# Router logits with the router's weights held in TensorE in two column tiles and the tokens streaming

## The chip, the cores and the metric

The kernel runs on one core of one Trainium2 chip. The metric is the time of one execution on the device, in microseconds (us), as the median of several runs.

## What is computed

One layer of a decoder trunk for 256 tokens of 2048 channels in fp32: two token mixers, a cross-attention into 256 memory tokens, a mixture of 32 experts, and a final norm. The part that matters here is the router ahead of the experts:

```python
p_grp = jax.nn.softmax((hn @ w_rg + b_rg), axis=-1)          # 4 groups
g_top = jnp.argmax(p_grp, axis=-1)
e_logits = (hn @ w_re + b_re).reshape(-1, N_GROUPS, EXPERTS_PER_GROUP)   # 32 experts
e_in = jnp.take_along_axis(e_logits, g_top[:, None, None], axis=1)[:, 0]
top_p, top_e = lax.top_k(jax.nn.softmax(e_in, axis=-1), TOPK_IN_GROUP)
```

`hn` is the normed residual, 256 x 2048. The 4 + 32 logits of every token come from one product of 2048 x 36 weights. Each token then goes through two experts (2048 x 512 gate and up, 512 x 2048 down).

## The kernel before

The dense products of the first part hold 128 x 128 tiles of the activations in TensorE and stream 512 weight columns, three products for each pair of tiles (high and low halves, lines 246 to 248, in `k_steps`). The weights come by DMA from Sync's queue (`wload`, line 163) and are split by ScalarE (L178) and VectorE (L179). The last dense stage is the output projection of the cross-attention: four slabs of 512 channels, each finished by `fin_co` (line 896), which

- adds the slab to the residual on VectorE (L902),
- turns it into channel-major tiles with eight transposes on TensorE (`turn`, L759),
- multiplies by the norm's gains on VectorE into `NT[s]`, two instructions (L914),
- squares the residual on ScalarE (L753) for the norm's sum,
- and calls `logits(s)` for the slab's four blocks of 128 channels.

In `logits` (line 889) the tokens are stationary and the router's 36 columns stream: for each of 16 blocks of channels, two products (128 tokens each) add to `lp[:, i * 36:i * 36 + 36]`, one PSUM bank with tokens on the partitions. An fp32 product is two load and two multiply instructions in the trace, so a slab has 16 of each.

After the four slabs VectorE sums the squares and makes `r2`, the inverse norm (L937 and `rstd_of`, lines 274 to 282, with one square root on ScalarE). L950 multiplies the raw logits by `r2` and adds the bias `br`, into `lg`. Line 952 and the loop behind it are products whose results nobody reads (`WARM` of them). A chain of small VectorE instructions picks the group and the experts (lines 958 to 984), three bf16 products rank the tokens (L988 to L990), `slot` is the place of each token in its expert, and `gather_unit` (line 1069) multiplies the residual by a 0/1 matrix, so that each group of four experts gets its tokens (L1080, L1081). Then the experts' gate and up products start (L1148): four column tiles of 32 tokens, each its own expert and half, 512 weight columns streaming. They read weights from seven large buffers and some borrowed ones; a buffer's next load goes out when its last product is done.

The order of instructions on each engine is made by a scheduler when the kernel is built, from the order of the program and its own estimates of when operands are ready. It moves instructions past each other, so the logits of a slab can stand between transposes of the next. `pump` (line 90) counts the PSUM banks of the tag `att`; `lp` takes one of four at line 884. The banks of the tag `acc` go round among the slabs, `wp`, `rk` and the experts. The first pool, `cst`, holds the constants (lines 184 to 192), and the pools behind it on the same side (`big`, `wpool`, `wleft` and others) begin where it ends, with padding tiles of fixed sizes between (lines 151 and 152). `load_small` (line 194) issues the constants' loads on Sync's queue while the first slab runs.

Of the kernel before, what the change touches and what calls it, by code (L numbers as in the profile page):

```python
# [13 lines left out]
F32 = mybir.dt.float32  # L14
# [4 lines left out]
OP = mybir.AluOpType  # L19
AX = mybir.AxisListType  # L20

P = 128
D = 2048
T = 256
# [109 lines left out]
def tile_block(ctx: ExitStack, tc: tile.TileContext, A, out, stop=None, dbg=None):  # L134
    nc = tc.nc
    mm = nc.tensor.matmul
    V, S = nc.vector, nc.scalar
# [4 lines left out]
    cst = ctx.enter_context(tc.tile_pool(name="cst", bufs=1))  # L142
# [27 lines left out]
    def psum(tag, name="pt"):  # L170
        return ps.tile([P, 512], F32, name=name, tag=tag)

    def tok(i):
        return slice(i * P, (i + 1) * P)
# [14 lines left out]
    peT = cst.tile([P, 2, 32], F32, name="peT")  # L189
    w2 = cst.tile([P, 2, P], F32, name="w2")  # L190
    wr = cst.tile([P, 16, 36], F32, name="wr")
    br = cst.tile([P, 36], F32, name="br")

    def load_small():
        nc.sync.dma_start(ct, A["cst"])
        nc.sync.dma_start(ctb, A["cstb"])
        nc.sync.dma_start(pos_i, A["pos"])
        nc.sync.dma_start(peT, A["peT"])
        nc.sync.dma_start(w2, A["w2"])
        nc.sync.dma_start(gw, A["w_g"])  # L200
        nc.sync.dma_start(wr, A["w_r"])
        nc.sync.dma_start(br, A["b_r"].to_broadcast([P, 36]))

    def C(n):
# [67 lines left out]
    def rstd_of(ss, name, keep):  # L272
        v = sm.tile([P, 2], F32, name="rv")
        V.tensor_scalar(v, ss, 1.0 / D, EPS, op0=OP.mult, op1=OP.add)  # L274
        r = keep.tile([P, 2], F32, name=name)
        S.activation(r, v, AF.Sqrt)  # L276
        V.reciprocal(r, r)  # L277
        t = sm.tile([P, 2], F32, name="rt")
        V.tensor_tensor(t, r, r, op=OP.mult)  # L279
        V.tensor_tensor(t, t, v, op=OP.mult)  # L280
        V.tensor_scalar(t, t, -0.5, 1.5, op0=OP.mult, op1=OP.add)  # L281
        V.tensor_tensor(r, r, t, op=OP.mult)  # L282
        return r
# [16 lines left out]
    identb, causb, strb, befb, oneb, aheadb = (ctb[:, x * P:x * P + P] for x in range(6))  # L300
# [581 lines left out]
    S.activation(s2, s2, AF.Sqrt)  # L882
    pump.banks -= 1
    lp = psum("att", "lp")
    X2 = X1

    NT = []

    def logits(s):
        for j in range(4):  # L890
            k = 4 * s + j
            for i in range(2):
                mm(lp[:, i * 36:i * 36 + 36], NT[s][:, j, tok(i)], wr[:, k], start=k + i == 0, stop=k == 15,
                   skip_group_check=True)

    def fin_co(s):
        xr = X2[s]

        def fin(acc):
            for c in parts if s == 3 else whole:  # L900
                for i in range(2):
                    V.tensor_tensor(xr[:, i, c], xr[:, i, c], acc[i][:, c], op=OP.add)  # L902
            if s == 3:
                squares(xr, ss2, s, acc)
            yield
            NT.append(a4([P, 4, T], F32, "nt"))
            yield from pump.take(2)
            TP = [turn(xr, pr) for pr in range(2)]
            if s == 3:
                logits(2)  # L910
            else:
                yield
            for pr in range(2):
                V.tensor_tensor(NT[s][:, 2 * pr:2 * pr + 2], TP[pr],  # L914
                                gains[:, 3, 4 * s + 2 * pr:4 * s + 2 * pr + 2, None].to_broadcast([P, 2, T]), op=OP.mult)
            pump.give(2)
            if s < 3:
                squares(xr, ss2, s, acc)
            if s != 2:
                yield  # L920
                logits(s)
        return fin
# [12 lines left out]
    mo = ctx.enter_context(tc.tile_pool(name="mo", bufs=1))  # L935
    s2 = sm.tile([P, 2], F32, name="s2")
    V.tensor_reduce(out=s2, in_=ss2, axis=AX.X, op=OP.add)  # L937
    r2 = rstd_of(s2, "r2", cst)
# [3 lines left out]
    def r_(shape, name):  # L942
        return rt.tile(shape, F32, name=name)
# [2 lines left out]
        return ap.unsqueeze(axis).to_broadcast(shape)  # L946

    lg = r_([P, 2, 36], "lg")
    for i in range(2):
        V.scalar_tensor_tensor(lg[:, i], lp[:, i * 36:i * 36 + 36], r2[:, i:i + 1], br, op0=OP.mult, op1=OP.add)  # L950
    wp = psum("acc", "wp")
    mm(wp[:36, :72], lg[:, 0], lg.rearrange("p i e -> p (i e)"), start=True, stop=True)
    for _ in range(WARM):
# [29 lines left out]
    for i in range(2):  # L983
        V.scalar_tensor_tensor(sel[:, i], bc(place[:, i], 1, [P, 4, 8]), 2.0, bc(og[:, i], 2, [P, 4, 8]),
                               op0=OP.is_lt, op1=OP.mult)
# [51 lines left out]
    if stop == "front":  # L1037
        combine()
        for s in every:
            nc.sync.dma_start(dbg["x2"][:, :, s], X2[s])  # L1040
        nc.sync.dma_start(dbg["lg"], lg)
# [27 lines left out]
    def gather_unit(g, u):  # L1069
# [8 lines left out]
        for a in range(4):  # L1078
            for i in range(2):
                mm(gp[:, a], X2[u][:, i, tok(a)], pg_[:, i].rearrange("p e s -> p (e s)"), start=i == 0, stop=i == 1)  # L1080
        V.tensor_tensor(L[u // 2][:, 4 * (u % 2):4 * (u % 2) + 4], gp,  # L1081
                        gains[:, 3, 4 * u:4 * u + 4, None].to_broadcast([P, 4, P]), op=OP.mult)

    def scatter(g, pT, ds, s, c):
        if len(YS) == s:
            YS.append(a4([P, 2, 512], F32, "y"))
        for i in range(2):
            yp = psum("att", "yp")[:, c]
            for x in range(2):
                mm(yp, pT[:, i], ds[:, x], start=x == 0, stop=x == 1)  # L1090
            V.tensor_tensor(YS[s][:, i, c], (X2 if g == 0 else YS)[s][:, i, c], yp, op=OP.add)
        if g == NG - 1:
# [40 lines left out]
    for g in range(NG):  # L1133
# [4 lines left out]
        for y in range(2):  # L1138
            gu = psum("acc", "gu")
            for q in every:  # L1140
# [3 lines left out]
                for j in range(4):  # L1144
                    k = 4 * q + j
                    for b in range(4):
                        e = 2 * y + b // 2
                        mm(gu[SL * b:SL * b + SL], XT[g][0][k // 8][:, k % 8, SL * e:SL * e + SL], w[b // 2](b % 2, j),  # L1148
                           start=k == 0, stop=k == 15)
# [43 lines left out]
    with tc.If(full > SL):  # L1193
# [8 lines left out]
        for q in range(4):  # L1202
            xt = a4([P, 4, T], F32, "xt")
            for j in range(4):
                gp = psum("att", "gx")
                for i in range(2):
                    mm(gp[:, tok(i)], X2[q][:, i, tok(j)], dg[:, i], start=True, stop=True)
                S.activation(xt[:, j], gp[:, :T], AF.Copy, scale=gains[:, 3, 4 * q + j:4 * q + j + 1])
# [5 lines left out]
        for x in range(2):  # L1214
            with tc.For_i(0, NE // 2, 1) as z:
                here = nc.values_load(pairs[0:1, bass.ds(z, 1), x], min_val=0, max_val=T)
                with tc.If(here > SL):
# [4 lines left out]
                    for q in range(4):  # L1222
                        w = wpool.tile([P, 8, 512], F32, name="w", tag="w")
                        nc.sync.dma_start(w, gu2[bass.ds(z, 1), x, q].rearrange("o p j c -> (o p) j c"))
                        for b in range(2):
                            for j in range(4):
                                for i in range(2):
                                    mm(gu[2 * b + i], XA[q][:, j, tok(i)], w[:, 4 * b + j],
                                       start=q + j == 0, stop=q + j == 6)
# [35 lines left out]
def layout(inputs):  # L1265
    f = {k: np.asarray(v) for k, v in inputs.items()}
    cc = np.ascontiguousarray

    def slabs(w, cols):
        k = w.shape[0] // 512  # L1270
        return np.stack([cc(w[:, c:c + 512].reshape(k, 4, P, 512).transpose(0, 2, 1, 3)) for c in cols])

    def halves(x):
        return cc(x.reshape(2, P, 2, 1024).transpose(1, 2, 0, 3))

    def tr(x):
        return cc(x.T.reshape(4, 4, P, T).transpose(0, 2, 1, 3))

    x, mem, w_in = f["x"][0], f["mem"][0], f["w_in"][0]
    every = range(0, D, 512)  # L1280
    w_in, w_bra, w_brb, w_o = (slabs(w, c) for w, c in (
        (w_in, _IN_ORDER), (f["w_br_nsa"][0], every), (f["w_br_sb"][0], every), (f["w_o"][0], every)))
    cq, ck, cv = (slabs(f[n][0], [0])[0] for n in ("w_cq", "w_ck", "w_cv"))
    co = slabs(f["w_co"][0], every)
    order = [w_in[s, q] for q in range(4) for s in range(2)]
    order += [w_in[s, q] for s in (4, 2, 3, 5, 6, 7, 8, 9, 10, 11, 12, 13, 14) for q in range(4)]
    order += [w_bra[s, q] for s in range(4) for q in range(2)]
    for s in range(4):
        order += [w_in[15 + s, q] for q in range(4)] + [w_brb[s, q] for q in range(2)]
    order += [w[s, q] for w in (w_o,) for s in range(4) for q in range(4)]  # L1290
    order += [w[q] for w in (cq, ck, cv) for q in range(4)] + [co[s, 0] for s in range(4)]
    dense = np.stack([np.concatenate(order[n:n + 2], 1) for n in range(0, len(order), 2)])
    eg, eu, ed = f["w_eg"][0].reshape(NE, D, 512), f["w_eu"][0].reshape(NE, D, 512), f["w_ed"][0].reshape(NE, 512, D)
    A = {
        "xT": tr(x), "memT": cc(tr(mem).transpose(1, 0, 2, 3)), "x_nat": halves(x), "mem_nat": halves(mem),
        "x_slab": cc(x.reshape(2, P, 4, 512).transpose(2, 1, 0, 3)),
        "pos": cc(f["positions"].reshape(2, P).T.astype(np.int32)),
        "gains": cc(np.stack([f[n][0].reshape(16, P).T for n in ("g_mix", "g_cross", "g_mem", "g_moe")], 1)),
        "dense": dense,
        "w_g": cc(f["w_in"][0][:, 2560:2584].reshape(16, P, 24).transpose(1, 0, 2)),  # L1300
        "peT": cc(np.stack([f["cmp_pe_k"][0].T, f["cmp_pe_v"][0].T], 1)),
        "w1": cc(np.stack([f[n][0].reshape(2, 16, P, P).transpose(0, 2, 1, 3)
                           for n in ("cmp_w1_k", "cmp_w1_v")])),
        "w2": cc(np.stack([f["cmp_w2_k"][0], f["cmp_w2_v"][0]], 1)),
        "w_r": cc(np.concatenate([f["w_rg"][0], f["w_re"][0]], 1).reshape(16, P, 36).transpose(1, 0, 2)),
        "b_r": cc(np.concatenate([f["b_rg"][0], f["b_re"][0]])[None]),
        "w_gu": cc(np.stack([eg, eu], 1).reshape(NE, 2, 4, 4, P, 512).transpose(0, 2, 4, 1, 3, 5)),
        "w_dn": cc(ed.reshape(NE // 2, 2, 4, P, 4, 512).transpose(0, 4, 3, 1, 2, 5)),
        "w_dl": cc(ed[NE - 4:, :, 1536:].reshape(4, 4, P, 2, 256).transpose(3, 2, 0, 1, 4)),
        "g_final": cc(f["g_final"][None]),  # L1310
        "cst": _CST_ARRAY, "cstb": _CSTB_ARRAY,
    }
    return A
# [15 lines left out]
```

## Time and profile before

| | |
|---|---|
| median of 3 runs | 1717.61 us (1717.32 to 1718.53) |
| the profiled execution's own time | 1717.69 us |
| its span, first to last instruction | 1715.8 us |
| mean granted TensorE clock | 0.926 |
| TensorE busy | 1432.6 us (83%) |
| VectorE busy | 558.6 us (33%) |
| ScalarE busy | 454.4 us (26%) |
| read from memory | 548.52 MB, 321 GB/s over the span |

The span is some 1.9 us shorter than the execution's own time; what lies around it is not in the profile. Busy shares are averages over the whole span, and the two halves of this kernel differ, so they are to be read by stage. In the views, PE is TensorE's multiplying, PEld its loading of stationary tiles, DVE is VectorE, ACT ScalarE, SP Sync. A product's time in the trace is longer than its step, since neighbours overlap; the step is read from start to start.

### The profile page before, as it was taken

The numbers are of one execution on the slowest core, as the hardware profiler recorded it, in microseconds if no ns is written. First come the engines' busy times: TensorE is split into PE (matmuls) and PEld (weight loads), VectorE is DVE, ScalarE is ACT, GpSimd is POOL, SyncE is SP. The second block draws the span as 40 slices with busy tenths as digits, with TensorE's granted clock in tenths as the row PEclk, the third lists the DMA queues.
The fourth block names the chain that finished last, engine by engine and source line by source line (L and its number), as shares of the span: only waits on it lengthen the run. The fifth ranks groups of instructions, "written<-read, shape, count | busy, mean of one in ns | idle before, by whom it ended". The sixth has DMA issues, their size and how long they took to land. (4 is left out here: it accounts for less than half of the span.)

```text
span 1715.8 us, 17953 instructions
## 1 busy us (share of the span) xinstructions
PE 1432.6 (83%) x7603; PEld 852.7 (50%) x7605; DVE 558.6 (33%) x876; ACT 454.4 (26%) x672; POOL 17.1 (1%) x27
## 2 busy tenths in 40 slices
PE   9999999999999999999876865866757658768665
PEld 7787778888888888886421311312213213113111
DVE  5656554344555555664120110200201201102002
ACT  5535455554344445651000000000000000000002
POOL 0000000000000000000000000000000000000002
PEclk9999999999999999999987987888978988879888
DMA  9753424545555645868999999999999999999996
GB/s 357 307 197 148 144 102 148 188 156 196 197 196 182 229 180 195 320 233 318 430 430 431 431 429 432 429 433 429 431 430 431 431 430 430 430 431 431 430 432 264
DMA packets 43574, 551.84 MB, mean 322 GB/s; under 512 B 5344, under 2 KB 5856, under 8 KB 10592
## 3 DMA queue, kind: packets, MB, share of 16 engines
q1 hardware_dynamic: 42848, 548.53, 77.9%
q0 software_dynamic: 640, 2.11, 0.3%
q8 instruction: 61, 1.00, 0.2%
q14 instruction: 25, 0.20, 0.0%
HBM read 548.52 MB, written 2.10 MB: 321 GB/s over the span
## 5 line engine op out<-in xcount | busy, mean ns | idle before, releaser
L1148 PE MATMUL gu<-w,xt 128*32 128x512 f32 x1984 | 362.4, 792 | 192.7 <-DMA w<-in_w_gu 192.7
L179 DVE TENSOR_TENSOR wl<-w,wh 128x1024 fp32r<-128x1024 f32 (+1 forms) x250 | 303.2, 1216 | 254.9 <-ACT wh L178 251.0
L178 ACT CAST wh<-w 128x1024 fp32r<-128x1024 f32 (+1 forms) x250 | 260.3, 1044 | 294.2 <-PE acc L248 282.1
L1148 PEld LDWEIGHTS gu<-w,xt 128*32 128x32 f32 x1984 | 81.8, 137 | 452.8 <-DMA w<-in_w_gu 268.4
L246 PE MATMUL acc<-wh,xhi 128*128 128x512 f32 x672 | 270.6, 404 | 0.6 <-ACT wh L178 0.6
L247 PE MATMUL acc<-wl,xhi 128*128 128x512 f32 x672 | 263.6, 392 | 1.1 <-DVE wl L179 1.1
L248 PE MATMUL acc<-wh,xlo 128*128 128x512 f32 x672 | 263.4, 392 | 0.0
L1180 PE MATMUL dd<-w,h 128*32 128x512 f32 (+1 forms) x1056 | 157.0, 631 | 34.0 <-DMA w<-in_w_dn 34.0
L1165 DVE TENSOR_TENSOR h<-h,tp 128x256 f32<-128x256 f32 x16 | 6.7, 421 | 538.0 <-ACT h L1164 538.0
L1155 ACT COPY gs<-gu 128x512 f32<-128x512 f32 x16 | 9.4, 585 | 571.0 <-PE gu L1148 571.0
L246 PEld LDWEIGHTS acc<-wh,xhi 128*128 128x128 f32 x672 | 126.7, 189 | 30.5 <-issue 3.6
L247 PEld LDWEIGHTS acc<-wl,xhi 128*128 128x128 f32 x672 | 126.9, 189 | 27.7 <-DVE wl L179 2.6
L248 PEld LDWEIGHTS acc<-wh,xlo 128*128 128x128 f32 x672 | 126.6, 188 | 27.2
L1180 PEld LDWEIGHTS dd<-w,h 128*32 128x32 f32 x1056 | 37.6, 115 | 120.9 <-issue 73.3
L181 ACT ACTIVATE ds<-dd,cw 128x512 fp32r<-128x512 f32 (+1 forms) x33 | 22.2, 674 | 261.2 <-PE dd L1180 261.2
L182 DVE SCALAR_TENSOR_TENSOR ds<-dd,cw,ds 128x512 fp32r<-128x512 f32 (+1 forms) x33 | 24.2, 735 | 164.6 <-ACT ds L181 164.6
L1090 PE MATMUL yp<-ds,pT 128*128 128x512 f32 (+1 forms) x132 | 47.9, 443 | 26.3 <-ACT ds L181 25.3
L246 PE MATMUL acc<-wh,oh 128*128 128x512 f32 x160 | 63.0, 394 | 0.0
L247 PE MATMUL acc<-wl,oh 128*128 128x512 f32 x160 | 62.4, 390 | 0.0
L248 PE MATMUL acc<-wh,ol 128*128 128x512 f32 x160 | 62.4, 391 | 0.0
L1090 PEld LDWEIGHTS yp<-ds,pT 128*128 128x128 f32 x132 | 20.0, 190 | 72.2 <-ACT ds L181 54.5
L246 PE MATMUL acc<-wh,mh 128*128 128x512 f32 x128 | 50.6, 395 | 0.0
(322 smaller groups left out, 1169.0 us busy)
## 6 DMA issues: line engine op xcount, KB each, us to landing
w<-in_w_gu SPq DMA_DIRECT2D x124, 2048.0 KB, 26.4
w<-in_w_dn SPq DMA_DIRECT2D x62, 2048.0 KB, 26.4
w<-in_dense SPq DMA_DIRECT2D x61, 2048.0 KB, 7.8
wa<-in_w_gu SPq DMA_DIRECT2D x16, 512.0 KB, 11.8
PT<-in_w SPq DMA_DIRECT2D x4, 1024.0 KB, 5.1
w<-in_w_dl SPq DMA_DIRECT2D x2, 2048.0 KB, 26.6
w<-in_x_nat SPq DMA_DIRECT2D x1, 2048.0 KB, 11.3
x<-in_x_slab POOLq DMA_DIRECT2D x4, 512.0 KB, 8.2
```

The lines of the kernel that those rows point to most:

```text
L178: S.copy(hi, src)
L179: V.tensor_tensor(lo, src, hi.bitcast(F32), op=OP.subtract)
L181: S.activation(hi, src, AF.Copy, scale=scale)
L182: V.scalar_tensor_tensor(lo, src, scale, hi.bitcast(F32), op0=OP.mult, op1=OP.subtract)
L246: mm(acc[i], hi[:, j, tok(i)], wh[:, jj], start=q + j == 0, stop=False)
L247: mm(acc[i], hi[:, j, tok(i)], wl[:, jj], start=False, stop=False)
L248: mm(acc[i], lo[:, j, tok(i)], wh[:, jj], start=False, stop=last and j == 3)
L1090: mm(yp, pT[:, i], ds[:, x], start=x == 0, stop=x == 1)
L1148: mm(gu[SL * b:SL * b + SL], XT[g][0][k // 8][:, k % 8, SL * e:SL * e + SL], w[b // 2](b % 2, j), start=k == 0, stop=k == 15)
L1155: S.copy(gs, gu)
L1165: V.tensor_tensor(h, h, tp[:, :, :, 1], op=OP.mult)
L1180: mm(dd[SL * e:SL * e + SL], H[e // 2][:, f, e % 2], wd[e](f), start=f == 0, stop=f == 3)
```

## The change

The constant `fold36` is loaded beside the others: a 128 x 36 matrix with a one where the row modulo 64 equals the column. The bank `lp` is first written with zeros over all partitions and 256 columns by one bf16 product. In `logits` the roles are swapped: the router's 36 columns are stationary, the 256 tokens stream, and even blocks of channels go to partitions 0 to 35, odd ones to 64 to 99. So there are 16 products instead of 32. After the four slabs VectorE copies the 128 x 256 sums to SBUF (`both`, in the buffer that `cmp` and `pcm` use later), and two products with `fold36` add the two halves and bring the tokens back to the partitions, in a new bank `lt` from which L950's instruction reads.

```diff
+    fold36 = cst.tile([P, 36], F32, name="fold36")
     br = cst.tile([P, 36], F32, name="br")
...
         nc.sync.dma_start(wr, A["w_r"])
+        nc.sync.dma_start(fold36, A["fold36"])
         nc.sync.dma_start(br, A["b_r"].to_broadcast([P, 36]))
...
     lp = psum("att", "lp")
+    mm(lp[:, :T], identb, causb[:, 0:1].to_broadcast([P, T]), start=True, stop=False, skip_group_check=True)
     X2 = X1
...
             k = 4 * s + j
-            for i in range(2):
-                mm(lp[:, i * 36:i * 36 + 36], NT[s][:, j, tok(i)], wr[:, k], start=k + i == 0, stop=k == 15,
-                   skip_group_check=True)
+            b = 64 * (k % 2)
+            mm(lp[b:b + 36, :T], wr[:, k], NT[s][:, j], start=False, stop=k >= 14, skip_group_check=True)
...
     lg = r_([P, 2, 36], "lg")
+    both = mo.tile([P, T], F32, name="both", tag="pcm")
+    V.tensor_copy(both, lp[:, :T])
+    lt = psum("acc", "lt")
     for i in range(2):
-        V.scalar_tensor_tensor(lg[:, i], lp[:, i * 36:i * 36 + 36], r2[:, i:i + 1], br, op0=OP.mult, op1=OP.add)
+        mm(lt[:, i * 36:i * 36 + 36], both[:, tok(i)], fold36, start=True, stop=True)
+    for i in range(2):
+        V.scalar_tensor_tensor(lg[:, i], lt[:, i * 36:i * 36 + 36], r2[:, i:i + 1], br, op0=OP.mult, op1=OP.add)
...
+        "fold36": (np.arange(P)[:, None] % 64 == np.arange(36)).astype(np.float32),
```

## Rows read from the trace of the kernel before

**Rows 1.** The page: mean busy share of the transfer engines in 40 equal slices, in tenths.

```profile
DMA  9753424545555645868999999999999999999996
```

**Rows 2.** Busy time by stage: stretch, its length, engines, granted clock, DMA share, GB/s.

```profile
794.00:798.00 4.00, 2.42 (x14) 0.90 (x15) 3.37 (x14) 0.00 (x0) 0.00 (x0) 1.00 1.06 433
...
802.00:810.00 8.00, 8.00 (x75) 5.13 (x77) 2.07 (x3) 0.00 (x0) 0.00 (x0) 0.98 0.08 33
...
830.00:1700.00 870.00, 606.97 (x3552) 195.92 (x3548) 103.59 (x178) 44.22 (x81) 7.59 (x8) 0.86 1.00 428
```

**Rows 3.** Waits of TensorE from 830 to 1700 us: total, times, longest.

```profile
PE gu L1148 <- DMA w<-in_w_gu: 192.7, 68, 4.0
```

**Rows 4.** Order of time, 801 to 812 us: Sync's issues (start, length, engine, line).

```profile
809.59 0.80 SPq L163 DMA_DIRECT2D w<-in_w_gu  x2
```

**Rows 5.** Order of time around the first block of logits, TensorE.

```profile
771.42 0.39 PE L247 MATMUL acc<-wl,oh 128*128 128x512 f32 x1
...
771.65 0.39 PE L248 MATMUL acc<-wh,ol 128*128 128x512 f32 x1
...
771.88 1.87 PE L893 MATMUL lp<-wr,nt 128*128 128x36 f32 x16
...
773.58 0.48 PE L246 MATMUL acc<-wh,oh 128*128 128x512 f32 x1
```

**Rows 6.** Order of time: an earlier slab's transposes, then the last slab to the logits.

```profile
768.27 1.03 PE L759 MATMUL tp<-ct,x 128*128 128x128 f32 x8
...
787.73 1.43 DVE L902 TENSOR_TENSOR x<-x,acc 128x256 f32<-128x256 f32 x4 [1.21 <-PE acc L248]
...
788.37 0.76 PE L893 MATMUL lp<-wr,nt 128*128 128x36 f32 x6
...
789.10 0.98 PE L893 MATMUL lp<-wr,nt 128*128 128x36 f32 x8
...
790.48 1.29 DVE L914 TENSOR_TENSOR nt<-tp,gains 128x512 f32<-128x512 f32 x2 [1.32 <-PE tp L759]
...
791.23 1.98 PE L893 MATMUL lp<-wr,nt 128*128 128x36 f32 x16 [0.31 <-DVE nt L914]
...
793.11 0.16 DVE L282 TENSOR_TENSOR r<-r,rt 128x2 f32<-128x2 f32 x1
793.37 0.42 DVE L950 SCALAR_TENSOR_TENSOR lg<-lp,r,br 128x36 f32<-128x36 f32 x2
```

**Rows 7.** Order of time: two fp32 products of 256 columns; steps of four 32-column tiles.

```profile
757.71 1.03 PE L837 MATMUL sp<-kmT,qcT 128*128 128x256 f32 x4
...
806.38 0.13 PEld L1148 LDWEIGHTS gu<-w,xt 128*32 128x32 f32 x4 [0.30 <-issue]
806.81 0.13 PEld L1148 LDWEIGHTS gu<-w,xt 128*32 128x32 f32 x4 [0.30 <-issue]
```

**Rows 8.** Order of time: whole-array bf16 products behind a narrower product.

```profile
794.38 1.46 PE L954 MATMUL wp<-ctb 128*128 128x512 bf16 x6 [0.16 <-issue]
```

**Rows 9.** Order of time around the head gates' folding product, and a copy by VectorE.

```profile
61.45 0.28 PE L466 MATMUL gp<-xlo,gs 128*64 128x256 f32 x1
...
61.77 0.36 ACT L469 COPY gc<-gp 64x256 f32<-64x256 f32 x1 [4.17 <-PE gp L466]
61.99 0.42 DVE L355 COPY kswT<-tp 128x256 f32<-128x256 f32 x1 [3.13 <-PE tp L353]
...
62.32 0.63 PE L472 MATMUL gp<-ct,gc 64*128 64x32 f32 x4
```

**Rows 10.** Sync's issue of br; the longest of TensorE's waits up to 760 us.

```profile
36.57 0.33 SPq L202 DMA_DIRECT2D br<-in_b_r  x1
...
PE wp L651 <- POOL zt L648: 1.4, 1, 1.4
```

**Rows 11.** Busy time by stage around the gather, columns as in rows 2.

```profile
799.00:800.00 1.00, 1.00 (x6) 1.00 (x6) 0.73 (x6) 0.20 (x1) 0.00 (x0) 0.50 1.09 467
...
803.00:804.00 1.00, 1.00 (x11) 1.00 (x11) 0.15 (x1) 0.00 (x0) 0.00 (x0) 1.00 0.15 49
```

## The prediction, made before the change was run

> **What bounds the kernel now.** I read the page's DMA line first, then the busy time by stage, then the waits of the last stage, and last the order of time around the router. The DMA line [rows 1] shows two kernels in one: about 18 slices of 43 us in which the transfer engines are partly busy, and then a second half at full share. The table by stage [rows 2] says where the border lies and what happens on it. From 830 us to 1700 us the transfers run at share 1.00 and 428 GB/s while TensorE is busy 607 of 870 us; TensorE's largest wait there is for expert weights [rows 3]. So the second half lasts as long as its bytes take, and its end moves only if the stream of bytes starts earlier or later. It does start at a definite moment: between 802 and 810 us the share falls to 0.08, because every weight buffer is full, and the next load is issued at 809.59 us [rows 4], when the first expert's matmuls (L1148) have used up the first buffers. Those matmuls wait for the gathered tokens, the gather for the router's decision, the router for the logits. TensorE is busy all the time up to 788 us. So everything on the chain from the last dense slabs through the router to 809.59 us moves the end one for one, up to some 7 us in the good direction (then the stall of the transfers is used up). A change of over 0.2%, 3.4 us, is about what a measurement of this kernel can tell from none.
>
> **Where the logits lie on that chain.** Per 512 channels the kernel has eight products with the tokens stationary and 36 columns moving. The first block [rows 5] stands between two dense products: 771.65 to 773.58 us where two neighbours without it are 0.23 us apart, so it costs 1.70 us. The second block, at 779.82 us, has the same 16 instructions and the same length. The third lies in the way of the transposes of the last slab [rows 6]: these could start when the sums at L902 are there (four adds from 787.73 us, 0.36 us each, of which the first transposes need three), but six and then eight instructions of logits go ahead of most of them, and VectorE gets its first transposed tile only at 790.48 us. The fourth block (791.23 to 793.21 us) runs beside the chain that makes r2, which ends at 793.27 us; the logits line L950 starts at 793.37 us. The two sides end together, so speeding up one alone gives nothing at this place.
>
> **The change, part by part.** The sum is made against the profiled execution, 1717.69 us (span 1715.8 and 1.9 around it), 0.08 us above the median of 1717.61.
>
> First and second block: four products of 36 stationary columns with 256 moving tokens. A plain fp32 product with 256 columns has two instructions, and four of them take 1.03 us [rows 7], some 0.24 us each with their filling; four narrow tiles side by side step every 0.43 us for 512 columns [rows 7], so 0.215 us for 256. Eight instructions in two tiles are four steps, 0.86 to 0.95 us, if the tiles run side by side. TensorE goes from whole-array to 64-column products and back; the nearest row is L952 to L954, where TensorE idles 0.16 us [rows 8]. Twice that makes 0.86 to 1.27 us a block; I take 1.1, which saves 0.6 us a block and 1.2 us for both (bounds 0.8 and 1.7). The Trainium skill, TensorEngine Tiling (Array Packing), section Key Properties, says that a change of tiling mode drains TensorE, which speaks against inserting such blocks among whole-array products. It gives no time for it; the 0.16 us of idle time agree in kind, and without any drain the block would come out at 0.9 instead of 1.1 us.
>
> Third block: half the time in the way of the transposes. Eight transposes take 1.03 us in an earlier slab [rows 6]; with a block of 0.9 to 1.1 us after the first transpose, the first tile is ready around 789.7 us instead of 790.4. I take 0.65 us gained (0 if the order of issue stays as unlucky, 1.1 if the block moves behind the transposes, since the third add ends at 788.8 us and VectorE could then start near 789.4).
>
> Fourth block: its last two products step in 0.43 us behind VectorE's second L914, so the raw logits are there some 0.6 us after it and no longer at 1.4. This gains nothing by itself, since r2 takes 1.5 us from the same point (791.77 to 793.27 us) [rows 6].
>
> New tail: a copy of the 128x256 sums out of PSUM, two products with the constant, then L950 as before. The same pattern is in the trace for the head gates [rows 9]: the copy starts 0.32 us after the last product's start, the folding product 0.19 us after the copy's end, and its four instructions take 0.63 us. VectorE copies this shape in 0.42 us [rows 9]. The copy stands in VectorE's queue with the seven small r2 steps. If it slips in as soon as the sums are there (0.59 us after L914), r2 is 0.42 us later and the fold is done at 1.83 us, so L950 starts at 2.0 us instead of 1.6: 0.4 us lost. If it is queued behind r2, L950 starts at 1.54+0.42+0.19+0.63+0.1 = 2.9 us: 1.3 us lost. I take 0.8, a place in the middle. Behind the copy waits r2, behind the fold waits L950, and everything after it.
>
> The zeroing product: bf16, 256 columns. Six of 512 columns take 1.46 us [rows 8], 0.24 each, so 0.12 and no change of mode; I take 0.15 us (0.1 to 0.3 if it has to wait for its bank).
>
> At nothing: the extra load of 18 KB in front of br. Sync's queue stood still until 36.57 us there [rows 10]; the loads behind it come one issue later, 0.33 to 0.5 us. What hides it are the weights already loaded: up to 760 us TensorE waits for no transfer, its longest wait is the one at the start [rows 10]. Uncovered, it would cost that 0.5 us. The copy's buffer is the one of cmp (L978), which is written some 2 us later; the fold's bank is one of the four that the finished slabs leave.
>
> Sum: -1.2 - 0.65 + 0.8 + 0.15 = -0.9 us, so 1717.69 - 0.9 = **1716.8 us**. With all bounds good -1.7 - 1.1 + 0.4 + 0.1 = -2.3 (1715.4), all bad -0.8 + 0 + 1.3 + 0.3 = +0.8 (1718.5).
>
> **The rivals.** (1) The two column tiles do not run side by side. For it: every row of concurrent tiles here has four tiles of 32 columns, none two of 64; against it: those step exactly as if side by side. Then a block is eight steps, 1.72 to 1.9 us plus the mode changes, 0.2 us more than today, the third block gains nothing, the fourth ends 1.1 us after L914, and the tail costs 0.9: 0.4 + 0 + 0.9 + 0.15 = +1.4, 1719.1 us. This ends slower than before; it decides as soon as two blocks save less than tail and zeroing cost. Chance 0.15.
>
> (2) The clock. TensorE idles much between 794 and 799 us, the granted clock is 0.50 from 799 to 802 us and 1.00 from 803 [rows 2, 11]; the gather runs 6, 7 and 6 instructions a us there instead of 11. The 19 instructions of 799 to 802 us would take 1.7 us instead of 3, and some of 802 to 803 too: 1.4 us. If the shifted idle stretch escapes this, 1716.8 - 1.4 = 1715.4 us, chance 0.13. If, with 0.8 us more of small work ahead of the gather, the low clock lasts a second such stretch, 1718.2 us, chance 0.12. Neither is in the forecast, since the chain keeps its idle pieces and gains some matmuls in them.
>
> (3) Addresses. The constant takes 144 bytes a partition in the first pool, and everything allocated behind it on that side moves, the expert weight buffers among them, while the three padding tiles (L151) keep their sizes. A loss of 1% of the stream's rate, about what separates its slower from its faster slices, would be 0.01 x 895 us = +9 us, 1725.7 us. For it speaks only that the padding exists; no row shows a load slower for where it lands. The Trainium skill, DMA: Bandwidth & Descriptors, section How a descriptor splits into AXI transactions, says that a transfer that doesn't start on a 256-byte boundary has one more transaction, which would be such a mechanism; no run here shows it yet. Chance 0.05.
>
> **How the numbers follow.** Forecast 0.52 (its own range 1715.4 to 1718.5), rival 1 0.15, the clock 0.13 and 0.12, addresses 0.05, the rest 0.03 for what I don't see. The range 1714.6 to 1719.2 us holds the forecast, most of rival 1 and most of both clock cases, and leaves out the addresses. Faster by over 0.2% (below 1714.2) needs the escaped clock and nearly all good bounds: 0.08. Slower by over 0.2% (above 1721.0) is the addresses and the worst of rival 1 with the clock: 0.08. Within: 0.84.
>
> **What would show it.** Right: the blocks at L895 take about 1.1 us between dense products, with their instructions overlapping in pairs; the first L914 of the last slab comes 1.5 to 2 us earlier; L950 starts 1.9 to 2.9 us after the last L914 instead of 1.6; the first expert load after the stall is issued near 808.7 us; from there to the end nothing changes. Wrong: blocks of 1.7 us or more (rival 1), another stretch of clock 0.50 under the gather, or a rate in the last 870 us that differs from 428 GB/s.

## The result: 1.2% slower, and hardly any of it in the router

The changed kernel takes 1737.72 us (median of 5 runs, 1734.9 to 1737.76) against 1717.32 us (5 runs, 1716.55 to 1718.53): ratio 1.0116 with a 95% interval of 1.0105 to 1.0127. The forecast was 1716.8 us with a range up to 1719.2, so it was wrong, in sign and far outside the range. The profiled execution of after took 1737.76 us, its span is 1735.9 (before 1715.8).

The head of the page and its line of the transfer engines, after:

```profile
span 1735.9 us, 17900 instructions
...
DMA  9654334445545654768999999999999999999996
```

Beside [rows 1] the kernel still has two halves, a part that TensorE bounds and a part at full transfer share. The first question is which half grew. Busy time by stage (columns as in [rows 2]), one stretch from the middle of each half, before and then after:

```profile
400.00:600.00 200.00, 200.00 (x899) 165.50 (x898) 107.39 (x104) 86.35 (x90) 2.32 (x4) 1.00 0.55 201
...
900.00:1600.00 700.00, 488.87 (x2840) 158.40 (x2830) 82.19 (x140) 30.50 (x52) 0.99 (x2) 0.86 1.01 431
```

```profile
400.00:600.00 200.00, 200.00 (x872) 161.13 (x871) 102.53 (x97) 84.26 (x88) 1.80 (x3) 1.00 0.53 191
...
900.00:1600.00 700.00, 481.03 (x2818) 155.92 (x2822) 80.33 (x138) 29.81 (x51) 0.99 (x2) 0.87 1.01 428
...
830.00:1700.00 870.00, 604.05 (x3602) 196.01 (x3596) 101.75 (x180) 41.91 (x72) 3.47 (x4) 0.88 1.01 428
```

Both did. From 400 to 600 us TensorE is never idle in either kernel and its granted clock is 1.00 in both, but it begins 872 products where it began 899, 3% fewer. Nothing that the change edits runs there. Start to start, twelve dense products of 512 columns took 2.72 us before and 2.80 after (the median over unbroken runs of twelve, worked out from the records), and that holds from 60 to 760 us, except between 160 and 260 us, where hardly any twelve stand in a row. One such run, its first and its thirteenth start, before and then after:

```profile
500.81 0.39 PE L247 MATMUL acc<-wl,xhi 128*128 128x512 f32 x1
...
503.53 0.39 PE L247 MATMUL acc<-wl,xhi 128*128 128x512 f32 x1
```

```profile
500.23 0.40 PE L248 MATMUL acc<-wh,oh 128*128 128x512 f32 x1
...
503.03 0.40 PE L248 MATMUL acc<-wh,xhi 128*128 128x512 f32 x1
```

In the second half the stream moves 428 instead of 431 GB/s. The window that the prediction meant to look at, 830 to 1700 us, shows 428 in both kernels: that of before [rows 2] takes in more of the stream's end. A window for a rate must lie inside the stream in both kernels.

The page's list of groups shows the first effect poorly, before and then after:

```profile
L246 PE MATMUL acc<-wh,xhi 128*128 128x512 f32 x672 | 270.6, 404 | 0.6 <-ACT wh L178 0.6
```

```profile
L248 PE MATMUL acc<-wh,xhi 128*128 128x512 f32 x672 | 274.4, 410 | 1.9 <-ACT wh L178 1.9
```

The mean of one rose by 6 ns, or 1.4%: neighbours overlap, so a record is longer than a step, and only the count in a saturated window, or start to start, tells the step.

Now the router. Order of time in after, TensorE around one block of logits, then the last slab to the experts:

```profile
789.88 0.40 PE L250 MATMUL acc<-wh,ol 128*128 128x512 f32 x1
790.21 1.06 PE L896 MATMUL lp<-nt,wr 128*36 128x256 f32 x8
...
791.20 0.50 PE L248 MATMUL acc<-wh,oh 128*128 128x512 f32 x1
...
805.21 0.40 PE L250 MATMUL acc<-wh,ol 128*128 128x512 f32 x1
...
805.69 0.62 PE L896 MATMUL lp<-nt,wr 128*36 128x256 f32 x2
...
806.50 0.63 PE L896 MATMUL lp<-nt,wr 128*36 128x256 f32 x4
...
807.06 0.64 PEld L761 LDWEIGHTS tp<-ct,x 128*128 128x128 f32 x6 [0.41 <-issue]
...
807.64 1.29 DVE L916 TENSOR_TENSOR nt<-tp,gains 128x512 f32<-128x512 f32 x2 [1.24 <-PE tp L761]
...
809.66 0.42 DVE L952 COPY both<-lp 128x256 f32<-128x256 f32 x1
...
810.19 0.60 PE L955 MATMUL lt<-fold,both 128*128 128x36 f32 x4 [0.57 <-issue]
...
810.85 0.42 DVE L957 SCALAR_TENSOR_TENSOR lg<-lt,r,br 128x36 f32<-128x36 f32 x2
...
816.16 4.29 PE L1087 MATMUL gx<-pg__5962,x 128*128 128x128 f32 x36 [0.85 <-DVE pg__5962 L1074]
820.37 7.07 PE L1155 MATMUL gu<-w,xt 128*32 128x512 f32 x64
...
824.04 0.80 SPq L163 DMA_DIRECT2D w<-in_w_gu  x2
```

A block costs 791.20 - 789.88 - 0.23 = 1.09 us, where it cost 1.70 [rows 5]. From the end of the second gains product (808.93) to the logits line are 1.92 us (before 1.60, [rows 6]), since the copy stands between two r2 steps and the fold runs beside the rest of them. Then comes something that the prediction had left alone: from the logits line to the first expert product are 9.52 us (820.37 - 810.85) where there were 12.55 (793.37 in [rows 6], 805.92 in the trace). Only 36 of the gather's instructions stand ahead of the experts now, 48 did before, and they ran at a granted clock of 1.00.

The account, by moments of the two profiled executions: the 247th of the 250 weight splits on VectorE starts 17.9 us later (767.33 to 785.19), 3.9 of these us by the 19th split; the logits line is 17.5 us later (793.37 to 810.85); the first load after the stall 14.45 us later (809.59 [rows 4] to 824.04); the end of the span 20.1 us later. So the dense products lose some 14 us after the first 55, the start loses 3.9, the router's part gives 3.4 back, and the last stage loses 5.7. Two of these numbers hold more than the change. Of the 3.9 us at the start, 1.3 are there by the 18th split already, and the start varies that much without any cause on record: over the fourteen profiles of this document the 18th split begins between 49.3 and 51.8 us. Of the 3.4 given back, 1.6 are the clock under the gather, which was low in the profile of before [rows 11] (see e5).

### The profile page after: what moved, and what is told of

It reads as the page before. It is cut to its first block, busy times and chain, and to the rows that moved or that the text cites. A ratio compares the mean times of both kernels' runs of the same rounds, so it can differ in the third digit from the quotient of the medians.

```text
span 1735.9 us, 17900 instructions
## 1 busy us (share of the span) xinstructions
PE 1442.6 (83%) x7577; PEld 842.8 (49%) x7578; DVE 558.7 (32%) x877; ACT 453.8 (26%) x672; POOL 17.1 (1%) x27
## 5 line engine op out<-in xcount | busy, mean ns | idle before, releaser
L248 PE MATMUL acc<-wh,xhi 128*128 128x512 f32 x672 | 274.4, 410 | 1.9 <-ACT wh L178 1.9
L1097 PEld LDWEIGHTS yp<-ds,pT 128*128 128x128 f32 x132 | 19.8, 188 | 71.3 <-ACT ds L181 54.4
```

Of the source, the lines that this page charges most:

```text
L248: mm(acc[i], hi[:, j, tok(i)], wh[:, jj], start=q + j == 0, stop=False)
```

## The experiments

The theory after this reading: the constant's 36 columns, 144 bytes a partition for which the first pool keeps 160, push every buffer behind them to another place, and two things dislike the new places: TensorE's dense products and the transfers. The rivals: the router's new instructions, the extra load or the order of work that came with it. In this kernel the activations' halves (stationary) lie in `big`, the split weights `wh` and `wl` (streaming) in a pool on the other side behind `gapr`, and the loaded weights, those of the experts among them, in `wpool`, which follows `big`. That makes the three movable one by one through the padding tiles.

Twelve runs; "before" is the kernel before on the same chip. The counts and rates are those of the stretches 400 to 600 and 900 to 1600 us:

| run | what differs | us | ratio to before | products | GB/s |
|---|---|---|---|---|---|
| e1 | change, constant in the padding's place | 1716.16 | 1.0003 [0.9994, 1.0013] | 896 | 431 |
| e2 | before, all moved 160 bytes | 1736.5 | 1.0122 [1.0103, 1.014] | 871 | 428 |
| e3 | before, stationary moved alone | 1732.8 | 1.01 [1.0082, 1.0119] | 871 | 431 |
| e4 | before, loaded weights moved alone | 1720.91 | 1.0034 [1.0019, 1.0049] | 898 | 428 |
| e11 | before, streaming moved alone | 1733.62 | 1.0106 [1.0076, 1.0135] | 868 | 430 |
| e12 | before, both operands (and loaded weights) moved | 1721.43 | 1.0027 [1.0015, 1.0039] | 899 | 428 |
| e10 | before, all moved 64 bytes | 1737.06 | 1.0126 [1.0096, 1.0155] | 872 | 428 |
| e8 | before, all moved 128 bytes | 1732.99 | 1.01 [1.0082, 1.0119] | 875 | 428 |
| e9 | before, all moved 256 bytes | 1716.49 | 1.0007 [0.9995, 1.0018] | 898 | 431 |
| e6 | before, with the extra load only | 1718.22 | 1.001 [1.0001, 1.0019] | 897 | 431 |
| e5 | change, constant among the others | 1714.15 | 0.9989 [0.998, 0.9998] | 899 | 431 |
| e7 | e5 with one column tile | 1714.81 | 0.9992 [0.9983, 1.0002] | 899 | 431 |

"All moved" means all pools behind the first padding tile on that side; the streaming pool stays. The five kernels of the table that lose 1% or more have two executions each, e4 three, the others seven to eleven. In e11 one of the seven large expert buffers and a borrowed one move along, which fits its 430 GB/s.

**e1: the change with everything else where it was.** Against the changed kernel:

```diff
-    for pool, n in ((gap, 40), (gap2, 80), (gapr, 56)):
+    for pool, n in ((gap2, 80), (gapr, 56)):
...
-    fold36 = cst.tile([P, 36], F32, name="fold36")
+    fold36 = gap.tile([P, 36], F32, name="fold36")
```

> The changed kernel with its constant put into the place of the first padding tile (160 bytes a partition), so that every buffer behind it starts where it did before the change. Theory A (start addresses): the dense products step at 0.227 us again, the transfers of the last stage run at some 429.7 GB/s, and what is left is the router itself, which the two traces put at 3 us gained: 1713 to 1716 us. Theory B (the changed instructions, their order, or the extra load cost the time): 1733 to 1738 us as in the changed kernel.

1716.16 us against 1715.9 for before. The 20 us are gone though every instruction of the change is still there. By stage:

```profile
400.00:600.00 200.00, 200.00 (x896) 165.48 (x896) 106.78 (x104) 86.16 (x90) 2.33 (x4) 1.00 0.55 201
...
900.00:1600.00 700.00, 484.95 (x2836) 158.08 (x2828) 82.18 (x140) 30.53 (x52) 0.99 (x2) 0.87 1.01 431
```

Both numbers are back at those of before. The places, not the instructions, make the loss. The gain of some 3 us that was expected of the router doesn't show; e6 and e5 look for it.

**e2: the places without the change.** The kernel before, its first padding tile 160 bytes larger:

```diff
-    for pool, n in ((gap, 40), (gap2, 80), (gapr, 56)):
+    for pool, n in ((gap, 80), (gap2, 80), (gapr, 56)):
```

> The kernel before with 160 bytes a partition more in the first padding tile and nothing else changed. Theory A: dense step 0.233 us, slower transfers, and without the router's gain 1737 to 1742 us. Theory B: 1716 to 1719 us.

```profile
400.00:600.00 200.00, 200.00 (x871) 161.15 (x870) 102.47 (x97) 83.40 (x87) 2.33 (x4) 1.00 0.53 190
...
900.00:1600.00 700.00, 480.91 (x2820) 157.48 (x2818) 82.08 (x141) 29.81 (x51) 0.99 (x2) 0.87 1.01 428
```

1736.5 us: 160 bytes that nobody reads cost 1.2%, and the stages are those of after.

**e3 and e4: which buffers.** In e3 `big` moves by 160 bytes and a second pad of 352 puts `wpool` and what follows 512 bytes further; in e4 `big` stays and the pools from `wpool` on move by 160.

```diff
     big = ctx.enter_context(tc.tile_pool(name="big", bufs=21))
+    gapb = ctx.enter_context(tc.tile_pool(name="gapb", bufs=1))
...
-    for pool, n in ((gap, 40), (gap2, 80), (gapr, 56)):
+    for pool, n in ((gap, 80), (gapb, 88), (gap2, 80), (gapr, 56)):
```

```diff
+    gapb = ctx.enter_context(tc.tile_pool(name="gapb", bufs=1))
...
-    for pool, n in ((gap, 40), (gap2, 80), (gapr, 56)):
+    for pool, n in ((gap, 40), (gapb, 40), (gap2, 80), (gapr, 56)):
```

> The kernel before with the pool of the activations (stationary in the dense products) moved by 160 bytes and every later pool moved by 512 bytes in all. If the dense step depends on where the stationary operand starts: step 0.233 us, 14 to 18 us lost there, transfers at 429.7 GB/s, 1731 to 1736 us. If it is the weight buffers that matter: 1716 to 1719 us.

> The kernel before with the activations' pool in its old place and the weight buffers and all later pools moved by 160 bytes. If transfers depend on where they land: dense step 0.227 us, transfers of the last stage at 427.6 GB/s instead of 429.7, 1720 to 1723 us. If the stationary operand were the only cause: 1716 to 1719 us.

By stage, e3 and then e4:

```profile
400.00:600.00 200.00, 200.00 (x871) 161.13 (x871) 102.33 (x97) 84.11 (x88) 2.32 (x4) 1.00 0.52 189
...
900.00:1600.00 700.00, 485.46 (x2836) 157.98 (x2838) 82.08 (x141) 29.81 (x51) 0.99 (x2) 0.86 1.01 431
```

```profile
400.00:600.00 200.00, 200.00 (x898) 165.47 (x897) 107.03 (x104) 85.85 (x90) 2.32 (x4) 1.00 0.55 201
...
900.00:1600.00 700.00, 487.08 (x2840) 157.28 (x2832) 82.18 (x140) 30.50 (x52) 0.99 (x2) 0.86 1.01 428
```

The two effects come apart cleanly: e3 has the slow products with the fast stream (+1.0%), e4 the fast products with the slow stream (+0.34%). Together they make e2's 1.2% within the intervals.

**e11 and e12: a place, or a distance?** If a place of `big` were bad in itself, moving the streaming pool alone would cost nothing, and moving both would stay slow. In e11 only `gapr` shrinks by 160 bytes, so the split weights move alone; in e12 `gap` grows by 160 as well. Read from opposite ends of the memory, these two moves go the same way.

```diff
-    for pool, n in ((gap, 40), (gap2, 80), (gapr, 56)):
+    for pool, n in ((gap, 40), (gap2, 80), (gapr, 16)):
```

```diff
-    for pool, n in ((gap, 40), (gap2, 80), (gapr, 56)):
+    for pool, n in ((gap, 80), (gap2, 80), (gapr, 16)):
```

> The kernel before with the pool of the split weights (which stream in the dense products, on the other side of the memory) moved by 160 bytes, the activations in their place; one of the seven large expert buffers and a borrowed one move with it. If the streaming operand's start counts as the stationary one's does: dense step about 0.233 us, 1730 us or more. If only the stationary operand counts: step 0.227 us and the transfers between 429 and 430 GB/s, 1715 to 1719 us.

> The kernel before with the activations' side moved by 160 bytes and the split weights' side by 160 bytes in the same direction, so that the two operands of a dense product lie as far from each other as before. If their distance counts: dense step 0.227 us, transfers 427.6 to 427.9 GB/s, 1720 to 1724 us. If each start counts by itself: step 0.233 us or more, 1736 us or more.

By stage, e11 and then e12:

```profile
400.00:600.00 200.00, 200.00 (x868) 161.05 (x867) 101.39 (x96) 84.30 (x88) 2.33 (x4) 1.00 0.52 188
...
900.00:1600.00 700.00, 483.17 (x2848) 157.81 (x2846) 82.11 (x141) 29.84 (x51) 0.99 (x2) 0.86 1.01 430
```

```profile
400.00:600.00 200.00, 200.00 (x899) 165.64 (x899) 107.47 (x104) 86.55 (x90) 2.33 (x4) 1.00 0.55 202
...
900.00:1600.00 700.00, 483.94 (x2828) 157.56 (x2826) 82.18 (x140) 30.52 (x52) 0.99 (x2) 0.87 1.01 428
```

It is the distance. Moving the streaming operand alone is as slow as moving the stationary one alone; moving both by the same amount restores 899 products. What e12 still loses (+0.27%) is the stream's part, as in e4, since its loaded weights moved too.

**e10, e8 and e9: what raster.** The first padding tile larger by 64, 128 and 256 bytes (56, 72 and 104 elements instead of 40), one kernel each; the diff is that of e10:

```diff
-    for pool, n in ((gap, 40), (gap2, 80), (gapr, 56)):
+    for pool, n in ((gap, 56), (gap2, 80), (gapr, 56)):
```

> The kernel before with 64 bytes more in the first padding tile. If any start off the good raster costs the same: transfers at 427.9 GB/s and a dense step of 0.232 to 0.2335 us, 1732 to 1737 us. If the loss grows with the distance: a step between 0.227 and 0.232 us, 1722 to 1731 us.

> The kernel before with 128 bytes a partition more in the first padding tile. If what counts is a multiple of 32 or 64 bytes: dense step 0.227 us, transfers at 430 GB/s, 1715 to 1718 us. If a 256-byte multiple counts for both: 1735 to 1738 us. If only the transfers want 256 bytes: dense step 0.227, transfers at 427.9 GB/s, 1719 to 1723 us.

> The kernel before with 256 bytes a partition more in the first padding tile. If what counts is the start modulo 256 bytes (128 more was slow in both respects): dense step 0.227 us, transfers at 430 GB/s, 1715 to 1718 us. If modulo 512 or the exact place: slow in one or both, 1720 us or more.

The products' stretch of e10, then both stretches of e8 and of e9:

```profile
400.00:600.00 200.00, 200.00 (x872) 161.39 (x871) 101.45 (x97) 84.90 (x89) 2.30 (x4) 1.00 0.53 191
```

```profile
400.00:600.00 200.00, 200.00 (x875) 162.37 (x874) 101.94 (x98) 84.06 (x87) 2.32 (x4) 1.00 0.53 193
...
900.00:1600.00 700.00, 486.77 (x2826) 156.59 (x2822) 79.47 (x135) 29.81 (x51) 0.99 (x2) 0.85 1.01 428
```

```profile
400.00:600.00 200.00, 200.00 (x898) 165.50 (x897) 107.42 (x104) 85.96 (x90) 2.33 (x4) 1.00 0.55 201
...
900.00:1600.00 700.00, 484.80 (x2836) 158.18 (x2832) 82.17 (x140) 30.52 (x52) 0.99 (x2) 0.86 1.01 431
```

64, 128 and 160 bytes are slow in both halves, 256 bytes in neither. 128 is a little less slow in the products than 64 or 160 (875 against 872 and 871). So a raster of 256 bytes fits all four distances; no other was tried, so a finer structure stays open.

**e6: the load alone.** The kernel before, with the constant loaded in the padding's place and read by nobody:

```diff
-    for pool, n in ((gap, 40), (gap2, 80), (gapr, 56)):
+    for pool, n in ((gap2, 80), (gapr, 56)):
...
+    fold36 = gap.tile([P, 36], F32, name="fold36")
...
+        nc.sync.dma_start(fold36, A["fold36"])
```

> The kernel before, its router unchanged, with the separate load of the constant alone (nobody reads it; it lies in the place of the first padding tile, so no buffer moves). Theory A2: ScalarE puts the first evacuation ahead of two weight casts, the 18th weight split comes some 2.5 us later, and the run is 1 to 2.5 us slower. Prediction's own price for this load: 0, at most 0.5 us.

1718.22 us against 1716.64, +1.6 us, an interval just above none. The 19th weight split starts 2.8 us later than before, though the 18th was only 0.2 later, and the 247th 2.1, so it is lost at the start and most of it stays lost. ScalarE in order of time, before and then e6:

```profile
50.95 1.99 ACT L178 CAST wh<-w 128x1024 fp32r<-128x1024 f32 x2
53.15 0.47 ACT L335 ACTIVATE nat<-acc,rx 128x256 f32<-128x256 f32 x1 [0.21 <-PE acc L248]
```

```profile
51.01 0.23 ACT L325 ACTIVATE cosx<-ang 128x32 f32<-128x32 f32 x1
...
53.34 0.47 ACT L337 ACTIVATE nat<-acc,rx 128x256 f32<-128x256 f32 x1 [2.10 <-PE acc L250]
53.72 1.98 ACT L178 CAST wh<-w 128x1024 fp32r<-128x1024 f32 x2
```

The load is not late and nobody waits for it. But with one load more the scheduler orders ScalarE otherwise: the evacuation of `nat` goes ahead of two casts, ScalarE waits 2.10 us for TensorE, and the casts, which feed TensorE, come 2.8 us later. In the changed kernel the same order is there, and TensorE waits 0.80 us for a cast and 0.54 us for the split behind it between 55 and 58 us.

**e5: the change without the load and without the move.** The constant is appended to the array of small constants, which is loaded anyway, and the padding tile shrinks to keep all places (on their raster):

```diff
     parts.append(("desc", np.broadcast_to(64.0 - np.arange(8), (P, 8))))
+    parts.append(("fold36", (p % 64 == np.arange(36)).astype(np.float32)))
...
-    for pool, n in ((gap, 40), (gap2, 80), (gapr, 56)):
+    for pool, n in ((gap, 8), (gap2, 80), (gapr, 56)):
...
-    fold36 = cst.tile([P, 36], F32, name="fold36")
...
-        nc.sync.dma_start(fold36, A["fold36"])
...
-        mm(lt[:, i * 36:i * 36 + 36], both[:, tok(i)], fold36, start=True, stop=True)
+        mm(lt[:, i * 36:i * 36 + 36], both[:, tok(i)], C("fold36"), start=True, stop=True)
```

> The changed router with every buffer where it was before the change and no load of its own for the constant: its 36 columns are appended to the block of constants that is loaded anyway, and the first padding tile shrinks by as much. Theory A2 (the separate load costs 2 us in the first 60 us, because ScalarE's order there differs with it; the router by itself gains some 2 us): the first 60 us as in the kernel before, 2 us faster than it and than the constant in the pad, 0.998 to 0.9995 of the time before. Rival (the two effects are chance of one profile): ratio 0.9995 to 1.001.

1714.15 us against 1716.64: 0.9989 [0.998, 0.9998]. That is what the change is worth without its load and its move, some 2 us gained, and the one version whose interval lies below before, if by little. In order of time, e5:

```profile
793.35 0.42 DVE L956 SCALAR_TENSOR_TENSOR lg<-lt,r,br 128x36 f32<-128x36 f32 x2
...
798.64 4.29 PE L1086 MATMUL gx<-pg__5960,x 128*128 128x128 f32 x36 [0.86 <-DVE pg__5960 L1073]
...
806.52 4.25 SPq L164 DMA_DIRECT2D w<-in_w_gu  x4
```

The logits line starts at 793.35 us, within 0.02 us of before [rows 6], but this execution came to the router later: its 247th weight split starts at 767.97 us, that of before at 767.33. Counted from there, the logits line comes 0.66 us earlier (25.38 against 26.04 us; in e1, where the split starts at 769.34 and the line at 794.67, 0.71). The next expert load goes out 3.1 us earlier than in [rows 4]. So most of the gain of this profile arises behind the logits. Two things make it, the number of gather instructions ahead of the experts and the clock under them. The gather in before, in e9 (with the router of before) and in e1, one line each:

```profile
798.77 7.23 PE L1080 MATMUL gx<-pg__5970,x 128*128 128x128 f32 x48 [0.95 <-DVE pg__5970 L1067]
...
799.20 5.60 PE L1080 MATMUL gx<-pg__5970,x 128*128 128x128 f32 x48 [0.53 <-DVE pg__5970 L1067]
...
799.96 5.91 PE L1087 MATMUL gx<-pg__5961,x 128*128 128x128 f32 x36 [0.85 <-DVE pg__5961 L1074]
```

Busy time by stage around the gather, e5 and then e1:

```profile
798.00:802.00 4.00, 3.36 (x30) 3.36 (x31) 3.56 (x20) 0.41 (x2) 0.00 (x0) 1.00 0.87 372
```

```profile
798.00:802.00 4.00, 2.78 (x17) 2.29 (x18) 3.29 (x21) 0.41 (x2) 0.00 (x0) 0.81 1.08 461
802.00:806.00 4.00, 4.00 (x31) 3.84 (x33) 2.01 (x5) 0.00 (x0) 0.00 (x0) 0.76 0.21 84
```

In e5, e1 and after, the scheduler puts 36 gather instructions ahead of the first experts instead of 48. Where the granted clock was 1.00, the upper of its two levels (2.4 GHz), 36 took 4.29 us (e5, and after) and 48 took 5.60 (e9). Where it was at the lower one (0.50, 1.2 GHz) for a while, 36 took 5.91 us (e1, a mean of 0.81 and 0.76 over the two stretches) and 48 took 7.23 (before). So the order gives 1.3 us and the clock 1.6. The clock differs between profiles with the same router: of the ten with the router of before, four have some 7.2 us here and five 5.6, with e6 between. What is left for the change in this profile is 0.66 and 1.3, some 2 us. Why the scheduler split the gather otherwise was not tried.

**e7: do the two column tiles run side by side?** e5 with all blocks of channels in one tile; the constant's lower half then only adds zeros.

```diff
-            b = 64 * (k % 2)
-            mm(lp[b:b + 36, :T], wr[:, k], NT[s][:, j], start=False, stop=k >= 14, skip_group_check=True)
+            b = 0
+            mm(lp[b:b + 36, :T], wr[:, k], NT[s][:, j], start=False, stop=k == 15, skip_group_check=True)
```

> As the merged constant, but all 16 router products in the column tile at 0, none at 64 (the constant's lower half then adds zeros). If two tiles run side by side: a block between dense products takes 1.8 to 2.0 us instead of 1.1, and the run is 1.5 to 3 us slower than with two tiles. If they don't: same block, same time.

TensorE in order of time, e7:

```profile
771.98 1.92 PE L895 MATMUL lp<-nt,wr 128*36 128x256 f32 x8
```

Eight instructions take 1.92 us in one tile and 1.06 us in two, so the two do run side by side. The expectation of 1.5 to 3 us for the whole kernel was missed: 1714.81 against 1714.15 us, with intervals that overlap. In the profiles e7's logits line does come 2.75 us later, counted from the 247th split (28.13 against 25.38 us). Only 28 instead of 36 gather instructions stand ahead of its experts, which gives a part back; where the rest goes is not shown.

## Why the prediction was wrong

- **The step that failed** is the third rival, "Addresses", and its sentence "For it speaks only that the padding exists". It had the cause, the constant's bytes and the padding that wasn't adjusted, but gave it 0.05 and looked for the loss in the transfers alone. Those lost 5 to 6 us, not 9 (e4: 5.0 us in the medians; 1720.91 - 1715.9). The larger part, 14 us, is in the dense products, and neither forecast nor rivals had a term for it: "TensorE is busy all the time up to 788 us" was read as if the stage could not change, and what sets the length of a step was not asked. A step 3% longer makes every stretch that consists of such steps 3% longer. (If each of the 2976 dense products of 512 columns lost 0.08/12 us, the estimate would be 19.8 us; 14 were lost, so not every step grew by that much.)
- **The bounds.** The forecast's terms were all of about 1 us, while the change moved the buffers of two stages of some 800 and 900 us. No row of before bounded that effect, and the sum took it at nothing instead of bounding it from both sides; the three padding tiles (L151) were the one sign in the code that places matter.
- **"At nothing: the extra load"** was 1.6 us in the medians (e6); e1 against e5, each measured against before, makes it some 2.7. The bound of 0.5 was taken from the loads behind it on Sync's queue; the price came through ScalarE's order, which was not looked at.
- **First and second block**: 1.1 us forecast, 1.09 measured, so the saving of 0.6 each was right. Rival 1, tiles one after the other, is refuted by e7. Four steps of 0.215 us would be 0.86, so some 0.2 us a block go with the entry and the exit. The Trainium skill, TensorEngine Tiling (Array Packing), section Key Properties, says that a change of tiling mode drains TensorE; this agrees with it in kind, but no run here separates the drain from the filling of the first product.
- **Third block**: 0.65 forecast, about 0.07 measured: the first gains product comes 2.43 us after the last dense product's start (807.64 - 805.21), where it came 2.50 us before (787.98 to 790.48 us). Two and then four instructions of logits stand between the transposes as six and eight did, so the lower bound ("if the order of issue stays as unlucky") was the case. The block that was to be half as long came in two groups: the first two instructions are one product in one tile and take 0.62 us alone, as long as the four behind them (0.63), and TensorE's next stationary load comes 0.41 us after the last one ([0.41 <-issue], 807.06 us).
- **Tail**: 0.8 forecast, 0.3 measured (1.92 against 1.60 us). It was the good bound of the two cases: the copy went in between two steps of r2 as soon as the sums were there, and the fold (810.19 to 810.79 us) ran beside the steps that remained.
- **The clock**, rival 2: the low stretch that stood under the gather is gone in after and e5 and there in e1, and it made 4.29 or 5.91 us of the same 36 instructions, 1.6 us, near the 1.4 that were given, and it differs between kernels with the same router (e5). The gather's new order, some 12 instructions fewer ahead of the experts, was not foreseen.
- Taken together, the router's part gives some 2 us (e5), where 0.9 was forecast: the right sign and half the size. Up to the logits line, which is what the sum was about, it gave 0.7, near the 0.9, but in part by luck: the third block gave 0.6 less than forecast and the tail cost 0.5 less. The rest comes from behind the logits line, where the sum had no term. And the sum left out the part that decides.

The Trainium skill, DMA: Bandwidth & Descriptors, section How a descriptor splits into AXI transactions, which the rival cited, says that a descriptor (one piece of a transfer) that does not start on a 256-byte boundary begins its first transaction at the boundary below. For pieces of 16 KB, as these loads have them, that is one transaction more. The runs agree with the direction and with the raster: 431 GB/s at 256 bytes, 428 at 64, 128 and 160. But the page speaks of what a transaction reads, and here the side that is written moved; whether the old places lie on such a boundary is not on record, and no row here counts transactions.

## What to carry to other kernels

A tile added to a pool is also a move of everything behind it: keep the old places when a constant is added (put it in a padding tile, or shrink one), and test the move alone before judging the change by its time. Where a saturated engine gets slower in a stage that the change doesn't touch, count its instructions in a fixed window at the same granted clock and look at the operands' places. A load that nobody waits for can still cost time, by changing the order that a scheduler makes elsewhere.

## What the hardware showed that was not expected

The step of a dense product (128x128 stationary, 512 columns, both in the kernel's split fp32 form) depends on where its two operands start relative to each other: 2.72 us for twelve when the distance is that of before or 256 bytes more, 2.79 to 2.81 us when the stationary operand is moved by 64, 128 or 160 bytes more or the streaming one by 160 alone, at a granted clock of 1.00 (2.4 GHz) in each. These are medians. The place of `big` or of the split weights is not bad in itself: with both moved by the same 160 bytes, twelve take 2.72 us again (e12). What in TensorE or in its reading of the memory makes it so is not shown.

Transfers into buffers that start off that raster run some 0.5% slower through the second half (299.89 against 301.43 MB between 900 and 1600 us, or 428 against 431 GB/s). Some 1.7 of the 5.7 us that the last stage lost arise only in its last 90 us (with 30 MB of loads left the lag is 18.4 us, at the end 20.1). These last 30 MB and what follows take 83.9 to 87.2 us in eight of the profiles (before, after, e1 to e4, e9 and e12), with the old places among both the short and the long ones, so the places need not be the cause; it stays open.
